# A two-block transformer kernel: second MLP, latents and output product with tokens in partitions

## The chip, the core and the metric

The kernel runs on one core of a Trainium2 chip. A core has a matrix engine (TensorE, PE in the rows; its weight loads are PEld), VectorE (DVE), ScalarE (ACT), GpSimd (POOL) and SyncE (SP), which issues most transfers. Each engine works through its own list of instructions in order; an instruction that waits holds back everything behind it on its engine. The metric is the device time of one execution in microseconds, median of several.

## The reference, cut to what matters

```python
def _mlp(h, w1, w2):
    a = jax.nn.relu(h @ w1)
    return (a * a) @ w2                                      # 1024 -> 4096 -> 1024
...
# end of the first block (two layers; tokens: 256)
        hx = hx + gx2 * _mlp(_modulate(hx, norm2_g[i], sx2, cx2), mlp_w1[i], mlp_w2[i])
    return _rms_norm(hx, final_g)
...
# second block, two layers
        mod = jax.nn.silu(c) @ w_ada[l] + b_ada[l]
        shift, scale, gate = jnp.split(mod, 3, axis=-1)
        h = x * (1.0 + scale[:, None, :]) + shift[:, None, :]
        (p_cq, p_ckv, p_kr, p_qb, p_kb, p_vb, p_qc, p_kc, p_vc,
         p_qi, p_ki, p_wi, p_gate) = jnp.split(h @ w_in[l], SPLIT_POINTS, axis=-1)
        cq = rms_norm(p_cq, q_norm_g[l])                     # 768 wide
        ckv = rms_norm(p_ckv, kv_norm_g[l])                  # 256 wide
        ...                                                  # mla, dilated and sparse attention
        y = jnp.concatenate([...], axis=-1) * jax.nn.silu(p_gate)
        sub = y @ w_out[l]
        x = layer_norm(ALPHA * x + (1.0 + gate[:, None, :]) * sub, ln_g[l], ln_b[l])
```

The sparse attention of a layer first scores all keys with eight small index heads (`p_qi`, `p_ki`, `p_wi`) and keeps the 64 best causal keys of each query.

## The kernel before

256 tokens are two tiles (t = 0, 1) of 128. Every product is made in three passes (`mm3`, L322 to L324): activations and weights are split in a high and a low part, and high·high, low·high and high·low are added in one accumulator. A weight piece of 128x1024 numbers arrives by DMA (`raw`, four buffers), ACT casts it to `whi` (L198) and DVE makes `wlo` (L201; keys that end in "+" on POOL instead); five buffers of each. The order in which pieces come is the list of `weight_plan`. `W.hold` names an instruction ahead of which no further `wlo` may be issued on DVE. A scheduler that places instructions by modelled times orders each engine's list, so that a piece's `wlo` can stand between two steps of a norm.

Activations stand with features in partitions (`hx`, `ahi`/`alo`: eight tiles of 128 features x 256 tokens) in most products: a weight block of 128x128 is stationary and 256 tokens move, or an activation block is stationary and 256 (384) weight columns move. The accumulators are PSUM banks: four of tag `mm`, two of `s`, one of `pt` and one of `om`.

The stages that the change touches, in order of time:

- `mlp(1)`, the second MLP: for each of eight groups of 512 hidden features two halves of the first product (`narrow`), a squared ReLU, then four weight pieces whose products go, 256 columns each, to eight accumulations that DVE adds to `hx` (`resid`, L837).
- `block2_start`: 16 transposes turn `hx` to `xa` (tokens in partitions, for the residual); squares on ACT, added on POOL, summed over partitions by PE (`sq_stats`, L748); the rsqrt, a broadcast by PE (L725); then eight steps of `modulate` (L757), each split in `ahi`/`alo` (L369, L370). POOL scales `xa` (L1427, L1428).
- `block2_layer`, twice: (layer 1 only: `vb`); `misc` and `qi` (the index projections); `indexer`: 16 score matmuls (L1441), the scores on DVE (L1446 to L1452), then 16 rounds of `max` and `match_replace` (L1456, L1457) and `sel` (L1459). Behind it stand the latents `b2c` (4 x 48 matmuls; copied to `craw`, L1537), their statistics (L748, L1540, L336 to L353) and `chi`/`clo` (L1546, L367/L368); then `qb`, `kb` (six projections), in layer 0 `vb`, and the ten attention pairs (`block2_pair`, L1473 to L1492), between which further projections stand.
- the gate `b2g` (L1647 to L1649, `yh` on ACT, `yl` on POOL L368), with the rows for gate, scale and shift: read from DRAM, broadcast over partitions, and finished on POOL (`row`, L705, L707; L1635 to L1637).
- the output product `b2o`: `out_tok` with 256 columns of a weight piece moving, then the layer norm of a tile (`finish`), whose result is transposed (L1685) and split (L1689, L1690) for layer 1. Then POOL finishes the residual rows (L1717, four times).

## Time and profile before

| | us |
|---|---|
| median of three runs | 1458.37 (1454.1 to 1460.74) |
| the profiled execution: run, span | 1461.6, 1459.8 |
| PE busy | 1391.7 (95%) |
| DVE busy | 1048.5 (72%) |
| ACT busy | 643.8 (44%) |
| POOL busy | 294.3 (20%) |
| mean granted clock | 0.977 |
| chain that ended last, PE's share | 77% |

The first MLP lasts until about 625, the second from 853 to 1033, layer 0 of the second block from there to 1250, layer 1 to the end. A row of the timeline gives start, duration, engine, line, operation, output<-input, shape, count and in brackets the idle time of the engine before it and what ended it. Matmuls overlap, so the distance of two starts is the pace, not the printed duration. A time in a row counts from the span's start.

### The profile page before, as it was taken

Reading aid. Unit: us, or ns where it says so; the run is one execution under the profiler, and the core shown is the slowest. Engines: PE = TensorE matmul, PEld = TensorE weight load, DVE = VectorE, ACT = ScalarE, POOL = GpSimd, SP = SyncE. Lnnn points to the kernel's source line nnn. Section 1 sums busy time; section 2 is a strip of 40 time slices with the busy share of each in tenths; the row PEclk is TensorE's granted clock in tenths of the full one; section 3 lists DMA queues with packets and bytes.
Section 4 is the critical chain, followed back from the end, with each engine's and each line's share of the span. In section 5 each row is a group of like instructions: output and inputs, shape, how many; then the busy total and the mean of one; then the engine's idle time right before and its main releaser. Section 6 shows DMA issues by size and latency. Waiting matters only on the chain.

```text
span 1459.8 us, 24691 instructions
## 1 busy us (share of the span) xinstructions
PE 1391.7 (95%) x9585; PEld 1208.6 (83%) x9585; DVE 1048.5 (72%) x1958; ACT 643.8 (44%) x1229; POOL 294.3 (20%) x281
## 2 busy tenths in 40 slices
...
GB/s 314 282 73 181 173 202 41 59 101 200 163 240 269 282 299 253 270 170 105 73 75 100 59 157 190 177 197 174 113 166 193 116 191 139 137 131 204 87 156 73
DMA packets 198116, 240.32 MB, mean 165 GB/s; under 512 B 21071, under 2 KB 178544, under 8 KB 198000
## 3 DMA queue, kind: packets, MB, share of 16 engines
...
q0 software_dynamic: 512, 0.02, 0.0%
...
## 4 chain that ended last, share of the span: by engine, by line
PE 77%; DVE 11%; DMA 4%; issue 3%; POOL 2%; ACT 2%; SPq 0%; ACTq 0%; DVEq 0%; POOLq 0%
PE mm L322 21%; PE mm L323 20%; PE mm L324 20%; DMA adaw<-in_ada_w 2%; DVE wlo L201 2%; PE om L1080 2%; PE s L1473 2%; PE pt L1065 1%; PE om L1490 1%; PE mm L502 1%; PE om L1333 1%; PE s L1014 1%; PE om L748 1%; PE pt L1484 1%; DVE acc L534 1%
## 5 line engine op out<-in xcount | busy, mean ns | idle before, releaser
L201 DVE TENSOR_TENSOR wlo<-raw,whi 128x1024 fp32r<-128x1024 f32 (+3 forms) x278 | 358.8, 1300 | 132.2 <-ACT whi L198 123.2
L198 ACT CAST whi<-raw 128x1024 fp32r<-128x1024 f32 (+3 forms) x282 | 289.2, 1035 | 334.5 <-PE mm L323 263.0
L322 PE MATMUL mm<-ahi,whi 128*128 128x256 f32 (+2 forms) x1232 | 398.5, 324 | 2.3 <-ACT ahi L369 2.3
L323 PE MATMUL mm<-alo,whi 128*128 128x256 f32 (+1 forms) x1232 | 395.1, 321 | 3.2 <-DVE alo L370 3.1
L324 PE MATMUL mm<-ahi,wlo 128*128 128x256 f32 (+1 forms) x1232 | 394.2, 321 | 0.0
L322 PEld LDWEIGHTS mm<-ahi,whi 128*128 128x128 f32 (+1 forms) x1232 | 237.5, 193 | 24.3 <-issue 3.9
L323 PEld LDWEIGHTS mm<-alo,whi 128*128 128x128 f32 x1232 | 237.4, 193 | 21.0 <-DVE alo L370 4.0
L324 PEld LDWEIGHTS mm<-ahi,wlo 128*128 128x128 f32 x1232 | 237.1, 193 | 18.5 <-issue 2.2
L322 PE MATMUL mm<-hid,whi 128*128 128x256 f32 (+1 forms) x544 | 179.4, 330 | 0.0
L323 PE MATMUL mm<-hid,whi 128*128 128x256 f32 (+1 forms) x544 | 178.8, 329 | 0.0
L324 PE MATMUL mm<-hid,wlo 128*128 128x256 f32 (+1 forms) x544 | 178.4, 328 | 0.0
L368 POOL TENSOR_TENSOR hid<-e,hid 128x512 fp32r<-128x512 f32 x48 | 78.0, 1626 | 417.1 <-ACT hid L367 417.1
L534 DVE SCALAR_TENSOR_TENSOR acc<-adaw,cst,acc 128x1024 f32<-128x1024 f32 x98 | 125.1, 1291 | 0.4
L322 PEld LDWEIGHTS mm<-hid,whi 128*128 128x128 f32 x544 | 103.0, 189 | 10.6 <-ACT whi L198 0.4
L324 PEld LDWEIGHTS mm<-hid,wlo 128*128 128x128 f32 x544 | 103.2, 190 | 10.0
L323 PEld LDWEIGHTS mm<-hid,whi 128*128 128x128 f32 x544 | 103.0, 189 | 9.6
L837 DVE SCALAR_TENSOR_TENSOR hx<-mm,cst,hx 128x256 f32<-128x256 f32 x160 | 72.4, 479 | 30.7 <-PE mm L324 30.4
L322 PE MATMUL mm<-whi,ahi 128*128 128x256 f32 (+1 forms) x192 | 57.4, 299 | 0.7 <-ACT ahi L1689 0.7
L324 PE MATMUL mm<-whi,alo 128*128 128x256 f32 (+1 forms) x192 | 56.1, 292 | 1.4 <-DVE alo L1690 1.4
L1136 ACT ACTIVATE e<-mm 128x512 f32<-128x512 f32 x48 | 28.7, 598 | 64.2 <-PE mm L324 62.2
L1138 DVE SCALAR_TENSOR_TENSOR e<-mm,e 128x512 f32<-128x512 f32 x48 | 32.9, 686 | 32.7 <-ACT e L1136 32.5
L323 PE MATMUL mm<-wlo,ahi 128*128 128x256 f32 (+1 forms) x192 | 55.9, 291 | 0.0
...
## 6 DMA issues: line engine op xcount, KB each, us to landing
raw<-in_mlp_w SPq DMA_DIRECT2D x128, 512.0 KB, 4.8
...
```

What stands on the lines that cost most here:

```text
L198: self.nc.scalar.copy(hi[:, :m], raw)
L201: (self.nc.gpsimd if on_pool else self.nc.vector).tensor_tensor(lo[:, :m], raw, hi[:, :m].bitcast(F32), op=OP.subtract)
L322: mm(ps, w[0], x[0], start=start, stop=False, skip_group_check=skip)
L323: mm(ps, w[0], x[1], start=False, stop=False, skip_group_check=skip)
L324: mm(ps, w[1], x[0], start=False, stop=stop, skip_group_check=skip)
L368: return (lo_eng or nc.vector).tensor_tensor(lo, t, hf, op=OP.subtract)
L534: V.scalar_tensor_tensor(acc, raw, s, acc, op0=OP.mult, op1=OP.add)
L837: self.nc.vector.scalar_tensor_tensor(h[m], ps, self.adaT[l][:, base + m, r:r + 1], h[m], op0=OP.mult, op1=OP.add)
L1080: nc.tensor.matmul(o[64 * hh:64 * hh + 64, cols(qt)], self.v[ab][:, 4 - nkt + i, cols(j // 2, 64)], PT[:, i, hh], start=i == 0, stop=i == ...
L1136: nc.scalar.activation(r, ps, AF.Relu)
L1138: V.scalar_tensor_tensor(t, ps, 0.0, r, op0=OP.max, op1=OP.mult)
L1473: nc.tensor.matmul(s[:, c0:c0 + n], qf(h, cols(qt)), kf(h, slice(0, n)), start=True, stop=True)
```

## The change

The MLP's and the second block's weight pieces become 256 rows x 512 columns. In `mlp1` a block of 128 hidden features x 128 tokens is stationary and 512 weight columns move, into four accumulators (two tiles x two halves) that stay open over all eight groups, in the four `mm` banks; the first product uses the two `s` banks. The residual `xt` is made token by token in the first group (the 16 transposes), gate, shift and scale come as broadcast rows, and their biases are added where the rows are made (`ada_jobs`: POOL fills a tile by up to 8 small DMAs, DVE adds, 4 to 8 small DMAs write the rows out). The last group and the final norm go tile by tile. In a layer of the second block, `b2c`, `vb` and `vc` come first, tokens stationary, 512, 384 and 256 columns moving; tile 1 follows tile 0 by three pieces (`LAG`). The latents' norm is worked per tile of tokens (squares on ACT, `latents`), and called behind `indexer`. The output product moves 512 columns, and `finish(t)` stands behind each tile's last product in both layers. `vb`'s low parts are made on DVE in both layers. The row additions of a layer (L705, L707) are gone.

```diff
-                for g in range(4):
-                    add(f"m{l}w2", w2, e * 512 - 512, 4, g * 256, 256)
+                for i in range(4):
+                    if l:
+                        add(f"m{l}w2", w2, e * 512 - 512 + 256 * (i // 2), 2, i % 2 * 512, 512)
...
+        for g in range(2):
             for i in range(4):
-                add("b2vb" + "+" * l, w, 256 * i, 2, 1824, 384)
+                add("b2c", w, 256 * i, 2, 512 * g, 512)
+        for i in range(4):
+            add("b2vb", w, 256 * i, 2, 1824, 384)
+        group("b2vc", w, 2720)
...
+                if rows:
+                    b = self.e([128, 256])
+                    nc.gpsimd.memset(b, 0.0)
+                    for i, key, bias in rows:
+                        for j in range(4):
+                            nc.gpsimd.dma_start(b[32 * j + i:32 * j + i + 1], bias[256 * j:256 * j + 256].unsqueeze(0))
+                    g2 = self.e([128, 256])
+                    nc.vector.scalar_tensor_tensor(g2, gt, plus, b, op0=OP.add, op1=OP.add)
...
-        nc.gpsimd.tensor_tensor(r, r, b, op=OP.add)
-        if plus:
-            nc.gpsimd.tensor_scalar(r, r, plus, 0.0, op0=OP.add, op1=OP.add)
...
+                self.mm3(acc[t][i % 2], (hh[:, kk, cols(t)], hl[:, kk, cols(t)]), (wh[:, k], wl[:, k]),
+                         e == 0 and kk == 0, e == 7 and kk == 3)
...
+            for i in (0, 2, 1, 3):
+                product(7, i, t, ws[i])
+            ss = self.sm([128, 2])
+            x = xt[t]
+            z = self.k4([128, 1024], name="z")
+            for i in range(2):
+                c = cols(i, 512)
+                V.tensor_tensor(z[:, c], acc[t][i], gate[:, c], op=OP.mult)
+                V.tensor_tensor(x[:, c], z[:, c], x[:, c], op=OP.add)
+                nc.scalar.activation(z[:, c], x[:, c], AF.Square, accum_out=ss[:, i:i + 1])
+            s1 = self.sm([128, 1])
+            V.tensor_tensor(s1, ss[:, 0:1], ss[:, 1:2], op=OP.add)
+            rstd = self.rsqrt(s1, 1, 1.0 / D, 1e-6, True)
+            for i in range(2):
+                c = cols(i, 512)
+                V.scalar_tensor_tensor(z[:, c], x[:, c], rstd, gr[:, c], op0=OP.mult, op1=OP.mult)
+                V.tensor_tensor(z[:, c], z[:, c], sr[:, c], op=OP.add)
+                self.turn_input(z[:, c], i, t, hi4, lo4)
+            with self.tc.issue_after(self.pow.ins):
+                nc.gpsimd.tensor_scalar(x, x, rstd, ALPHA, op0=OP.mult, op1=OP.mult)
+                nc.gpsimd.tensor_tensor(x, x, fr, op=OP.mult)
...
+    def turn_input(self, u, i, t, hi4, lo4):
+        nc = self.nc
+        pt = self.psum("pt", [128, 4, 128])
+        for k in range(4):
+            nc.tensor.transpose(pt[:, k], u[:, cols(k)], self.ident)
+        hv, lv = (f[i][:, :, cols(t)] for f in (hi4, lo4))
+        self.last_hi = nc.scalar.copy(hv, pt)
+        op = nc.vector.tensor_tensor(lv, pt, hv.bitcast(F32), op=OP.subtract)
+        if i == 0:
+            self.W.hold = op.ins
...
+        gain = self.k4([128, 1024], name="lgain")
+        self.after(gain, xa[0])
...
+        def token_step(i, t, w):
+            key, k0, nk, n = steps[i]
+            if k0 == 0:
+                pss[t, key] = self.psum("mm" if key < 2 else "s", [128, n])
+            ps = pss[t, key]
+            for k in range(nk):
+                kk = k0 + k
+                self.mm3(ps, (a[0][kk][:, cols(t)], a[1][kk][:, cols(t)]), (w[0][:, k], w[1][:, k]), kk == 0, kk == 7)
...
+                c = cols(key, 512)
+                V.tensor_tensor(lat[t][:, c], ps, gain[:, c], op=OP.mult)
+                junk = self.e()
+                for j in range(key + 1):
+                    cc = slice(256 * j, 256 * j + 512 // (key + 1))
+                    nc.scalar.activation(junk[:, cc], ps[:, cc], AF.Square, accum_out=cst[t][:, key + j:key + j + 1])
+        steps = ([(g, 2 * i, 2, 512) for g in range(2) for i in range(4)] + [(2, 2 * i, 2, 384) for i in range(4)]
+                 + [(3, 4 * i, 4, 256) for i in range(2)])
+        LAG, ws = 3, {}
+        for i in range(len(steps) + LAG):
+            if i < len(steps):
+                ws[i] = self.W.get(("b2c", "b2c", "b2vb", "b2vc")[steps[i][0]])
+                token_step(i, 0, ws[i])
+            if i >= LAG:
+                token_step(i - LAG, 1, ws.pop(i - LAG))
...
+            r = self.rsqrt(s[:, 0:2], 2, 1.0 / 256, 1e-6, True)
+            u = lat[t]
+            V.tensor_scalar(u[:, 0:768], u[:, 0:768], r[:, 0:1], None, op0=OP.mult)
+            V.tensor_scalar(u[:, 768:1024], u[:, 768:1024], r[:, 1:2], None, op0=OP.mult)
+            for i in range(2):
+                pt = self.psum("pt", [128, 4, 128])
+                for k in range(4):
+                    nc.tensor.transpose(pt[:, k], u[:, 512 * i + 128 * k:512 * i + 128 * k + 128], self.ident)
+                hv, lv = (f[i][:, :, cols(t)] for f in (chi4, clo4))
+                nc.scalar.copy(hv, pt)
+                V.tensor_tensor(lv, pt, hv.bitcast(F32), op=OP.subtract)
...
         sel = self.indexer(l, qi, ki, wi)
-        craw = [self.k4([128, 4, 256], name="craw") for _ in range(2)]
...
+        for t in range(2):
+            latents(t)
...
+            tmp = self.k4([128, 1024], name="tmp")
+            nc.gpsimd.tensor_tensor(tmp, lnb, gr, op=OP.mult)
+            nc.gpsimd.tensor_tensor(gr, lng, gr, op=OP.mult)
+            nc.gpsimd.tensor_tensor(sr, tmp, sr, op=OP.add)
...
-        for gg in range(2):
-            ws = [[self.W.get("b2o") for _ in range(2)] for _ in range(2)]
+        for g in range(2):
+            ws = [self.W.get("b2o") for _ in range(4)]
             for t in range(2):
-                for g in range(2):
-                    out_tok(2 * gg + g, t, ws[g], self.psum("mm", [128, 256]))
-                if gg == 1 and l == 0:
+                out_tok(g, t, ws)
+                if g:
                     finish(t)
         if l == 1:
-            finish(0)
-            finish(1)
```

Between the scores of the indexer and the attention pairs (layer 0). On PE before, behind the last score (`s`, L1441) stands the first latent product (`mm_10878`):

```order
L1441 MATMUL s_10810<-misc_10627,qi_10642 128x128 [waits PE_49]
L1441 MATMUL s_10810<-misc_10627,qi_10642 128x256
L1441 MATMUL s_10817<-misc_10627,qi_10642 128x128 [waits Activation_49]
L1441 MATMUL s_10817<-misc_10627,qi_10642 128x256
L322 MATMUL mm_10878<-ahi_10554,whi_10708 128x256
L323 MATMUL mm_10878<-alo_10556,whi_10708 128x256
L324 MATMUL mm_10878<-ahi_10554,wlo_10709 128x256
L322 MATMUL mm_10878<-ahi_10554,whi_10708 128x256
L323 MATMUL mm_10878<-alo_10556,whi_10708 128x256
```

On PE now, behind the scores stand the projections; the last of the fourth (`mm_10921`, `kb`), then the transposes of the latents (`lat`, L1594), then the fifth:

```order
L320 MATMUL mm_10921<-ahi_10052,whi_10853 128x256
L321 MATMUL mm_10921<-alo_10054,whi_10853 128x256
L322 MATMUL mm_10921<-ahi_10052,wlo_10854 128x256
L1594 MATMUL pt_10778<-cst_61,lat_10177 128x128 [waits DVE_49,Activation_49]
L1594 MATMUL pt_10778<-cst_61,lat_10177 128x128 x3
L1594 MATMUL pt_10785<-cst_61,lat_10177 128x128 [waits DVE_49]
L1594 MATMUL pt_10785<-cst_61,lat_10177 128x128 x3
L320 MATMUL mm_10953<-ahi_10051,whi_10885 128x256
L321 MATMUL mm_10953<-alo_10053,whi_10885 128x256
L322 MATMUL mm_10953<-ahi_10051,wlo_10886 128x256
L320 MATMUL mm_10953<-ahi_10051,whi_10885 128x256
L1594 MATMUL pt_10801<-cst_61,lat_10178 128x128 x4
```

The four latent products have moved from behind the scores to ahead of them, and transposes that wait for DVE stand between the fourth and the fifth projection.

On DVE before, at the end of the indexer (`score`, `sel`), the statistics of the latents follow:

```order
L1457 MATCH_REPLACE score_10767<-sm_10868,score_10767 128x256 [waits DVE_49]
L1456 MAX sm_10871<-score_10767 128x8 [waits DVE_49]
L1457 MATCH_REPLACE score_10767<-sm_10871,score_10767 128x256 [waits DVE_49]
L1459 TENSOR_SCALAR sel_10874<-score_10767 128x384 [waits DVE_49]
L201 TENSOR_TENSOR wlo_11262<-raw_11065,whi_11261 128x1024 [waits DMAHW1_49,PE_49,Activation_49]
L1540 TENSOR_SCALAR sm_11126<-om_11127 128x2 [waits PE_49]
L201 TENSOR_TENSOR wlo_11294<-raw_11095,whi_11293 128x1024 [waits DMAHW2_49,Activation_49]
L1540 TENSOR_SCALAR sm_11126<-om_11153 128x2 [waits PE_49]
L336 TENSOR_SCALAR sm_11163<-sm_11126 128x4 [waits DVE_49]
```

On DVE now, the scaling of the latents (`lat`, L1589, L1590) follows the last rounds, and `clo` (L1597) follows both tiles' scaling:

```order
L1495 MAX sm_10761<-score_10660 128x8 [waits DVE_49]
L1496 MATCH_REPLACE score_10660<-sm_10761,score_10660 128x256 [waits DVE_49]
L1495 MAX sm_10764<-score_10660 128x8 [waits DVE_49]
L328 TENSOR_SCALAR sm_10772<-sm_10179 128x2
L1496 MATCH_REPLACE score_10660<-sm_10764,score_10660 128x256 [waits DVE_49]
L1589 TENSOR_SCALAR lat_10177<-lat_10177,sm_10774 128x768 [waits Pool_49]
L1498 TENSOR_SCALAR sel_10767<-score_10660 128x384 [waits DVE_49]
L1590 TENSOR_SCALAR lat_10177<-lat_10177,sm_10774 128x256
L328 TENSOR_SCALAR sm_10795<-sm_10180 128x2
L1589 TENSOR_SCALAR lat_10178<-lat_10178,sm_10797 128x768 [waits Pool_49]
L1590 TENSOR_SCALAR lat_10178<-lat_10178,sm_10797 128x256
L1597 TENSOR_TENSOR clo_10487<-pt_10778,chi_10485 128x4x128 [waits Activation_49]
L1597 TENSOR_TENSOR clo_10488<-pt_10785,chi_10486 128x4x128 [waits Activation_49]
```

Ahead of both stands the whole indexer; what PE waits for now comes out of DVE's list behind it.

At the gate of layer 0, on POOL, before: the rows' additions stand among the low parts `yl`:

```order
L705 TENSOR_TENSOR rows_12324<-rows_12324,rowb_12325 128x1024 [waits DMAHW3_49,DMAHW2_49,Pool_49]
L707 TENSOR_SCALAR rows_12324<-rows_12324 128x1024 [waits Pool_49]
L1635 TENSOR_TENSOR gsr_12339<-lgb_12318,rows_12324 128x1024 [waits DMAHW4_49,PE_49,Pool_49]
L1636 TENSOR_TENSOR gsr_12340<-lgb_12319,rows_12324 128x1024 [waits DMAHW5_49,PE_49]
L1707 TENSOR_SCALAR lgb_12319<-lgb_12319 128x1024 [waits Pool_49]
L368 TENSOR_TENSOR yl_12346<-e_12409,yh_12344 128x256 [waits DVE_49,Activation_49]
L368 TENSOR_TENSOR yl_12346<-e_12415,yh_12344 128x256 [waits Activation_49]
L705 TENSOR_TENSOR rows_12332<-rows_12332,rowb_12333 128x1024 [waits DMAHW1_49,DMAHW0_49]
L368 TENSOR_TENSOR yl_12346<-e_12482,yh_12344 128x256 [waits Activation_49]
L1637 TENSOR_TENSOR gsr_12340<-gsr_12340,rows_12332 128x1024 [waits Pool_49]
L368 TENSOR_TENSOR yl_12346<-e_12488,yh_12344 128x256 [waits Activation_49]
L368 TENSOR_TENSOR yl_12347<-e_12555,yh_12345 128x256 [waits Activation_49]
L368 TENSOR_TENSOR yl_12347<-e_12561,yh_12345 128x256 [waits Activation_49]
```

On POOL now:

```order
L1695 TENSOR_TENSOR tmp_11778<-rows_11769,rows_11772 128x1024 [waits DMAHW7_49,DMAHW0_49,Pool_49]
L1696 TENSOR_TENSOR rows_11772<-rows_11766,rows_11772 128x1024 [waits DMAHW1_49,Pool_49]
L1697 TENSOR_TENSOR rows_11775<-tmp_11778,rows_11775 128x1024 [waits DMAHW1_49]
L366 TENSOR_TENSOR yl_11784<-e_11847,yh_11782 128x256 [waits PE_49,Activation_49]
L366 TENSOR_TENSOR yl_11784<-e_11853,yh_11782 128x256 [waits Activation_49]
L1756 TENSOR_SCALAR rows_11769<-rows_11769 128x1024
L366 TENSOR_TENSOR yl_11784<-e_11920,yh_11782 128x256 [waits Activation_49]
L366 TENSOR_TENSOR yl_11784<-e_11926,yh_11782 128x256 [waits Activation_49]
```

Three long row additions (L1695 to L1697) are left, all ahead of the first `yl`.

At the boundary from the second MLP to layer 0, on DVE before: `modulate` and the split by feature tile, one row of 256 tokens each:

```order
L757 SCALAR_TENSOR_TENSOR e_10566<-hx0_133,sm_10552,om_10549 128x256 [waits Activation_49]
L370 SCALAR_TENSOR_TENSOR alo_10556<-e_10558,cst_61,ahi_10554 128x256 [waits Activation_49]
L370 SCALAR_TENSOR_TENSOR alo_10556<-e_10562,cst_61,ahi_10554 128x256 [waits Activation_49]
L757 SCALAR_TENSOR_TENSOR e_10570<-hx0_133,sm_10552,om_10549 128x256
L757 SCALAR_TENSOR_TENSOR e_10574<-hx1_134,sm_10552,om_10549 128x256 [waits DVE_49]
L370 SCALAR_TENSOR_TENSOR alo_10556<-e_10566,cst_61,ahi_10554 128x256 [waits Activation_49]
L370 SCALAR_TENSOR_TENSOR alo_10556<-e_10570,cst_61,ahi_10554 128x256 [waits Activation_49]
L370 SCALAR_TENSOR_TENSOR alo_10557<-e_10574,cst_61,ahi_10555 128x256 [waits Activation_49]
L757 SCALAR_TENSOR_TENSOR e_10578<-hx1_134,sm_10552,om_10549 128x256
```

On DVE now: the end of tile 0's norm, all of tile 1's, and then the next pieces' low parts:

```order
L1236 TENSOR_TENSOR z_10080<-z_10080,rows_8564 128x512 [waits DVE_49] x2
L1251 TENSOR_TENSOR alo_10053<-pt_10095,ahi_10051 128x4x128 [waits Activation_49]
L1251 TENSOR_TENSOR alo_10054<-pt_10104,ahi_10052 128x4x128 [waits Activation_49]
L1227 TENSOR_TENSOR z_10138<-mm_8391,rows_8558 128x512
L1235 SCALAR_TENSOR_TENSOR z_10138<-xt_8530,sm_10149,rows_8567 128x512 [waits Pool_49]
L1235 SCALAR_TENSOR_TENSOR z_10138<-xt_8530,sm_10149,rows_8567 128x512
L1236 TENSOR_TENSOR z_10138<-z_10138,rows_8564 128x512 [waits DVE_49] x2
L1251 TENSOR_TENSOR alo_10053<-pt_10153,ahi_10051 128x4x128 [waits Activation_49]
L199 TENSOR_TENSOR wlo_10184<-raw_10033,whi_10183 128x1024 [waits DMAHW4_49]
L199 TENSOR_TENSOR wlo_10197<-raw_10039,whi_10196 128x1024 [waits DMAHW5_49]
L1251 TENSOR_TENSOR alo_10054<-pt_10162,ahi_10052 128x4x128 [waits Activation_49]
```

The norm of tile 1 stands behind that of tile 0, and the low parts of the third and fourth piece (`wlo_10184`, `wlo_10197`) behind tile 1's first `alo`.

## Rows read from the trace of the kernel before

**Rows 1.** Windows: stretch, length, each engine's busy time and instructions, clock, DMA share, GB/s.

```profile
416.30:438.60 22.30, 22.30 (x99) 18.00 (x97) 21.08 (x31) 5.85 (x8) 3.35 (x2) 1.00 0.74 238
900.00:1000.00 100.00, 100.00 (x844) 100.00 (x844) 65.43 (x82) 45.34 (x53) 15.85 (x9) 1.00 0.56 180
```

**Rows 2.** Windows, the same columns: from the scores of layer 1 to its first pair.

```profile
1287.00:1334.00 47.00, 46.72 (x400) 45.55 (x396) 40.85 (x104) 25.50 (x46) 11.25 (x11) 1.00 0.49 140
```

**Rows 3.** Timeline of PE: first scores of both layers, first pair of layer 1.

```profile
1063.17 0.93 PE L1441 MATMUL s<-misc,qi 64*128 64x128 f32 x8
...
1286.68 0.93 PE L1441 MATMUL s<-misc,qi 64*128 64x128 f32 x8
...
1334.02 0.49 PE L1473 MATMUL s<-qkb 64*128 64x128 f32 x4
```

**Rows 4.** Groups of DVE in 1066.2 to 1092.9: busy us, mean ns.

```profile
L201 DVE TENSOR_TENSOR wlo<-raw,whi 128x1024 fp32r<-128x1024 f32 x8 | 10.1, 1266 | 1.6 <-ACT whi L198 1.6
```

**Rows 5.** Timeline of DVE: the indexer's first and last operation, layer 0.

```profile
1066.28 0.55 DVE L1446 TENSOR_SCALAR score<-e,sm 128x128 f32<-128x128 f32 x2
...
1092.54 0.36 DVE L1459 TENSOR_SCALAR sel<-score 128x384 f32<-128x384 f32 x1
```

**Rows 6.** Groups of PE in 1286.6 to 1334.0: the scores.

```profile
L1441 PE MATMUL s<-misc,qi 64*128 64x128 f32 (+1 forms) x32 | 3.3, 340 | 0.0
```

**Rows 7.** Timeline: 512-wide steps of a norm on DVE, ACT and POOL.

```profile
1254.28 1.40 DVE L1676 SCALAR_TENSOR_TENSOR u<-z,sm,gsr 128x512 f32<-128x512 f32 x2
1258.94 0.59 ACT L1689 CAST ahi<-pt 128x512 fp32r<-128x512 f32 x1 [1.26 <-PE pt L1685]
1254.44 1.00 POOL L332 TENSOR_TENSOR sm<-sm,cst 128x1 f32<-128x1 f32 x1 [3.49 <-DVE sm L330]
```

**Rows 8.** Windows: before and after PE's longest idle time of layer 1's start.

```profile
1274.90:1280.70 5.80, 5.80 (x28) 4.99 (x29) 3.31 (x3) 1.05 (x1) 1.45 (x2) 0.58 0.38 122
1280.70:1286.60 5.90, 5.90 (x52) 5.85 (x50) 2.45 (x2) 3.54 (x4) 0.00 (x0) 1.00 0.68 188
```

**Rows 9.** Windows: MLP to layer 0, output product of layer 0, its norm, output product of layer 1.

```profile
1033.00:1063.00 30.00, 24.02 (x163) 22.22 (x161) 20.93 (x30) 14.16 (x24) 10.08 (x7) 0.77 0.18 51
1214.00:1250.00 36.00, 28.07 (x206) 26.86 (x205) 26.28 (x35) 11.49 (x19) 24.16 (x18) 0.86 0.39 107
1250.00:1287.00 37.00, 28.00 (x186) 25.80 (x186) 27.12 (x28) 15.67 (x21) 17.56 (x12) 0.91 0.49 147
...
1429.00:1452.00 23.00, 23.00 (x194) 22.84 (x193) 16.08 (x31) 4.83 (x8) 8.55 (x9) 1.00 0.08 29
```

**Rows 10.** Timeline of PE and POOL: gate rows of layer 0, and who waits.

```profile
1217.59 0.39 PE L324 MATMUL mm<-whi,yl 128*128 128x256 f32 x1 [2.07 <-POOL yl L368]
...
1221.75 0.58 PE L324 MATMUL mm<-whi,yl 128*128 128x256 f32 x1 [3.54 <-POOL yl L368]
...
1198.13 2.67 POOL L705 TENSOR_TENSOR rows<-rows,rowb 128x1024 f32<-128x1024 f32 x1 [4.90 <-DMA rowb<-in_b_ada]
1200.89 3.70 POOL L707 TENSOR_SCALAR rows<-rows 128x1024 f32<-128x1024 f32 x1
```

**Rows 11.** Timeline of POOL, DVE and PE: long POOL additions and what ran beside them.

```profile
1040.81 4.85 POOL L1428 TENSOR_TENSOR xa<-xa,fgrow 128x1024 f32<-128x1024 f32 x2
...
1041.06 4.88 DVE L370 SCALAR_TENSOR_TENSOR alo<-e,cst,ahi 128x256 fp32r<-128x256 f32 x2
...
1260.75 12.34 POOL L1717 TENSOR_TENSOR z<-z,lgb 128x1024 f32<-128x1024 f32 x4 [3.06 <-ACT z L1714]
...
1262.78 11.40 DVE L201 TENSOR_TENSOR wlo<-raw,whi 128x1024 fp32r<-128x1024 f32 x4 [2.52 <-ACT whi L198]
...
1274.89 1.06 PE L1724 MATMUL om<-misc,kc 32*32 32x256 f32 x2 [6.52 <-DVE sm L1525]
```

**Rows 12.** Timeline: the last column group's product on DVE; eight row DMAs on POOL.

```profile
1452.17 0.42 DVE L1664 TENSOR_TENSOR z<-mm,rows 128x256 f32<-128x256 f32 x1 [0.20 <-PE mm L324]
...
624.64 4.13 POOL L682 DMA_DIRECT2D row<-adag  x8 [19.19 <-ACT adag L544]
```

315 lines of the change are left out of this document (137 added, 178 removed).

## The prediction

> **What bounds the kernel now.** I read the windows first, since a share over the whole span says nothing of a stage. Inside the MLPs PE has no idle time and runs at full clock: 844 matmuls of 256 columns in 100 us, and 99 matmuls, nearly all of 512 columns, in 22.3 us [rows 1]. So there only PE's pace counts. The second block's layers are nearly as dense between the first scores and the first pair (46.72 of 47 us busy [rows 2]). Time is lost at three places: from the MLP to layer 0 (6 of 30 us idle, clock 0.77), around the output product of layer 0 (7.9 of 36 us idle, clock 0.86) and at layer 1's start (9 of 37 us idle, clock 0.91); the output product of layer 1 loses nothing [rows 9]. Such idle time costs twice: after a wait of 6.52 us [rows 11] the granted clock is 0.58 for 5.8 us, in which 28 matmuls go where 52 go in the next 5.9 us [rows 8], about 2.5 us more. I call T the start of PE's first score of a layer.
>
> **Parts that shorten. Wider matmuls:** 768 pairs of 256-column matmuls become one each (384 in the MLP, 192 in the latents, 192 in the output products). A pair takes 2 x 100/844 us = 0.237, one of 512 columns 0.232 on a run of 96 (by the window's 22.3/99, 0.225, as a few are smaller) [rows 1]: 5 ns each, **-4**; bounds -9 (0.225) and -2.
>
> The Trainium skill, page "TensorE: Matmul & The Clock Gate", section "Back-to-back issue gap", gives N/2.4 + 2.5 ns for a matmul of N columns, by which a pair would save 2.5 ns, so 2 us in all; the rows show both sizes slower than that. The same section has a sustained 131 ns at 512 columns, by which this part would save over 80 us and the kernel would end near 1377; the window's 22.3 us for 99 matmuls speaks against it, so it gets a chance of less than 1 in 100.
>
> **Gate rows.** 192 products of the output with all around them take 36 us in layer 0 and 23 in layer 1 [rows 9]. Of the 13, some 3 are the norm inside that stretch; 10 follow from the long row additions on POOL, which hold back `yl` (idle 2.07 and 3.54 us, and the low clock after them). Two additions and a scaling ahead of the first `yl` and one between them go (2.67, 3.70 and as much as 2.67 [rows 10]); three of about 2.4 us are left, which begin as the rows have landed, 1198 on this axis, and end some 7.5 us later, 9 us ahead of the first output product. I take **-8.5** (bounds -10 and -5), since wider products also reach the last `yl` sooner.
>
> **Tail.** Layer 1's last step on DVE works on 512 columns instead of 256: three operations of 0.70 [rows 7] for three of 0.42 [rows 12], **+0.8**. Tile 0's finish ends ahead of it either way.
>
> **Parts that move. MLP to layer 0.** The 16 residual transposes go into the MLP (16 x 0.12 = **+1.9** of PE there). Now 30 us hold 120 products of 0.119 (14.2), so 15.8 are lost [rows 9]. After: from the end of tile 0's product, tile 1's takes 24 x 0.232 = 5.6. Tile 0's norm on DVE: gate and residual of the second half 1.4, square 0.7, sums 0.3, a `wlo` 0.5 more, POOL's power 1.0, two scalings 1.4, then shifts 1.4 [rows 7]. But POOL's addition on the residual, 4.85/2 = 2.4, starts with them, and an operation of DVE with two SBUF inputs beside one took 4.88/2 instead of 0.42 [rows 11]: first transposes at 8.2 instead of 6. Tile 1's chain stands wholly behind it on DVE and meets the same: its first transposes come at about 20.8, while PE has run out at 13. The third and fourth pieces' `wlo` come behind that, and PE is steady from 27.4, having done 54 products (12.5): 14.9 lost, with 2.5 for the low clock 17.4, **+1.5** (bounds -4, without POOL's overlap, and +5).
>
> **Layer 0 to layer 1.** Now 37 us hold 48 products of 0.175 and 120 of 0.119 (22.6), so 14.4, and 3 us ahead of that: 17.4 lost. POOL makes no `wlo` any more, but its four additions (12.34) still hold DVE's `wlo` to 11.40/4 = 2.85 each [rows 11]. Worked out as above, PE is steady at 18.8 with 3.6 lost; then `lgain`, whose transfer waits for a POOL copy behind the third addition, lands about 31 and holds DVE's first latent row and the `wlo` behind it until 33, with 23.1 us of work done: 10 lost, with the products' starts and the clock 14. **-3** (bounds -11, if `lgain` is early, and +4).
>
> **Latent wait.** This is the largest term. Now the latent products, 192 of 0.119 = 22.8, stand behind the scores and cover the indexer on DVE, which lasts from T + 3.1 for 26.6 us [rows 3, 5]. After, only `qb` and three quarters of what follows stand there. PE: scores 3.3 [rows 6], four projections 96 x 0.119 = 11.4, so T + 14.7; then the transposes of `lat`. DVE: in the 26.6 us are six `wlo` of 1.27 (7.6 [rows 4]) and two copies like those of 0.70 (1.4 [rows 7]); 17.6 is the indexer. After, four `wlo` (5.1) stand in it, and tile 0's scaling comes behind the last round: 3.1 + 17.6 + 5.1 - 0.4 + 0.6 (768 columns, between 0.36 for 384 and 0.70) = T + 26.0. PE waits 11.3. The four turns share the one `pt` bank: each is 0.5 on PE, 0.59 on ACT and 0.70 on DVE [rows 7], and the first low part stands behind tile 1's scaling too, so they start at 26.0, 28.1, 29.9 and 31.7. Seventeen of the last 48 products fit between; 31 are left (3.7): first pair at T + 35.9, with the low clock T + 38.4. Work in it is 3.3 + 144 x 0.119 + 2.0 = 22.4, so 13.5 to 16 are lost. Against now: T to pair is 47.3 [rows 3], less 22.8 for the moved products leaves 24.5. So 11.4 to 13.9 per layer; layer 1's list reads the same. I take 13.5, **+27** for both (bounds +16, if the rounds need less and the clock stays, and +32). What could cover it, the attention pairs' own projections, stands behind the transposes on PE's list.
>
> **Smaller.** `vb` and `vc` only move (their products are as before). With tile 1 three pieces behind, four of five weight buffers are held; a freed one needs ACT 1.05 and DVE 1.27 plus waits, about 2.5, against 12 x 0.232 = 2.78 of products: hidden, but a latent row of 0.70 in between takes the rest; **+2** for both layers (0 to +6). The ada rows: bias DMAs like those of 0.5 us each [rows 12], most beside an MLP in which PE alone counts; the last four jobs' writes stand among the squares of a norm on POOL, **+1** (0 to +4).
>
> **Sum:** -4 - 8.5 + 0.8 + 1.9 + 1.5 - 3 + 27 + 2 + 1 = +18.7 on the profiled run's 1461.6, so 1480; that run lies 3.2 above the median of 1458.4, on whose scale I state **1477** (own range 1464 to 1490).
>
> **Rivals.** *The stalls' relief outweighs the latent wait (faster).* At the three lossy places the wait now ends on a long POOL addition. If DVE and PE there pass it (`lgain` early, POOL's additions not beside the norms), the terms are -4, -11 and -10 with -7 for the matmuls, and the latents stay at +16 as the rounds go back to back: -4 - 11 - 10 - 7 + 16 + 6 = -10, **1448**. It decides from about 24 us of gain at these places. For it: the rows show those losses really are there to be had; against it: all three still have a POOL addition beside DVE on the new list.
>
> *The wait is there but half covered (about the same).* If the four turns overlap and the clock recovers within the wait, 9 per layer: 18.7 - 9 = +9.7, and the boundaries at half their bounds give 9 back: **1459**. For it: ACT and DVE are otherwise free there.
>
> *Every piece waits (slower still).* If the lag leaves one free buffer while POOL holds DVE, a step takes 1.05 + 2.85 + waits, 4.1, against 2.78 for some eight steps in layer 1 and half of that in layer 0: +15 on the sum, **1490**.
>
> *The change does not do what it says:* the lists show fewer matmuls and the new order, so no chance of its own.
>
> **How the numbers follow.** Forecast 0.60, faster rival 0.18, same 0.14, slower still 0.08. About 0.5% (7.3 us) is what a measurement can tell from no change. Faster takes the first rival's 0.18, less its nearest part, 0.17; same 0.17, with the forecast's low edge; slower 0.66. The range reaches from 1450, half into the faster rival, to 1490.
>
> **What would show it.** In the new profile: PE idle of 9 to 13 us in each layer, put down to DVE's scaling of `lat` (L1589), at transposes L1594, and a clock near 0.6 behind it; the indexer on DVE about as long as now. The idle on `yl` gone. A first transposes' idle of about 7 us in tile 1 of the MLP's norm. 512-column matmuls at 0.232. The forecast is wrong if the scaling of `lat` stands free of the indexer, or if the first pair begins before T + 31.

## The result, and the profile after

The changed kernel takes 1475.5 us (median of four runs, 1473.97 to 1476.02) against 1459.41 for the kernel before beside it: a ratio of 1.012 with a 95% interval of 1.009 to 1.015. It is slower, 1.5 us from the forecast of 1477. The profiled execution took 1476.02 with a span of 1474.2, against 1461.6 and 1459.8 before, so 14.4 more. In the page PE is busy 8.8 us less than before (1382.9 for 1391.7) but stands still 23 us longer, and its mean granted clock is lower (0.970 for 0.977): PE waits longer and then runs slow.

First the windows of the changed kernel by stage, the columns as in [rows 1]: the second MLP; from it to layer 0's scores; scores to first pair; pairs to the output product; output product and norm to layer 1's scores; scores to first pair; pairs to the output product; its own stretch.

```profile
851.07:1034.74 183.67, 182.28 (x1163) 165.93 (x1164) 99.75 (x101) 90.29 (x113) 33.51 (x23) 0.98 0.60 195
1034.74:1102.68 67.94, 60.22 (x335) 51.84 (x333) 40.51 (x52) 27.36 (x48) 11.60 (x8) 0.90 0.56 157
1102.68:1140.76 38.08, 25.62 (x193) 24.04 (x192) 28.45 (x83) 13.28 (x24) 1.71 (x4) 0.82 0.27 82
1140.76:1229.31 88.55, 86.97 (x648) 72.58 (x648) 62.88 (x160) 48.00 (x122) 29.54 (x29) 1.00 0.45 147
1229.31:1317.99 88.68, 79.64 (x430) 66.79 (x428) 56.61 (x72) 38.81 (x60) 27.40 (x19) 0.98 0.58 167
1317.99:1355.95 37.96, 25.38 (x194) 23.81 (x193) 28.46 (x83) 13.39 (x24) 1.41 (x2) 0.82 0.20 65
1355.95:1442.92 86.97, 86.24 (x647) 72.52 (x647) 56.59 (x161) 49.27 (x125) 19.62 (x24) 1.00 0.45 146
1442.92:1464.70 21.78, 21.78 (x97) 17.84 (x96) 13.99 (x21) 4.82 (x8) 7.28 (x7) 1.00 0.07 25
```

The two rows from scores to first pair stand out: 12.5 us without work for PE in each, at a clock of 0.82, where the kernel before had next to none [rows 2]. The same borders in the trace of before:

```profile
848.10:1033.00 184.90, 184.84 (x1536) 184.55 (x1536) 121.66 (x156) 87.43 (x109) 32.20 (x23) 0.99 0.59 187
1033.00:1063.17 30.17, 24.19 (x164) 22.25 (x162) 21.10 (x30) 14.16 (x24) 10.08 (x7) 0.77 0.18 52
1063.17:1121.04 57.87, 57.29 (x449) 55.77 (x449) 45.36 (x109) 29.40 (x52) 9.15 (x13) 0.97 0.55 162
1121.04:1214.40 93.36, 92.22 (x696) 78.30 (x696) 65.60 (x160) 49.06 (x124) 38.71 (x34) 1.00 0.54 178
1214.40:1286.68 72.28, 55.36 (x382) 51.95 (x380) 52.94 (x61) 26.89 (x37) 41.33 (x28) 0.88 0.44 126
1286.68:1334.02 47.34, 47.06 (x402) 45.88 (x401) 41.01 (x104) 25.71 (x46) 11.25 (x11) 1.00 0.50 142
```

Products moved across these borders, so only stretches that hold the same work before and after can be set side by side. The second MLP's first product begins at 848.1 before, not at the 853 given above. The last column adds the prediction's terms by stretch, rounded:

| stretch | before | after | difference | by the prediction's terms |
|---|---|---|---|---|
| start to the second MLP's first product | 848.1 | 851.1 | +3.0 | +1 |
| second MLP | 184.9 | 183.7 | -1.2 | 0 |
| MLP's end to layer 0's output product | 181.4 | 194.6 | +13.2 | +15.5 |
| from there to layer 1's output product | 214.7 | 213.6 | -1.1 | +2 |
| that product and the tail | 30.7 | 31.3 | +0.5 | +0.3 |
| sum | | | +14.4 | +18.8 |

The waits of PE in the whole of the changed kernel (engine and line that waits, what ended the wait; total, how often, longest; waits of the first MLP and of the start left out):

```profile
PE pt L1594 <- DVE lat L1589: 21.3, 2, 10.7
PE mm L321 <- DVE wlo L199: 6.5, 4, 5.4
PE pt L1248 <- DVE z L1236: 5.9, 2, 4.6
...
PE pt L1594 <- DVE clo L1597: 3.7, 2, 1.9
```

The first line is the forecast's largest term. In the timeline of the changed kernel, PE's transposes of layer 0 and what DVE did ahead of them:

```profile
1126.65 0.41 DVE L1496 MATCH_REPLACE8 score<-sm,score 128x256 f32<-128x256 f32 x1
...
1127.50 0.62 DVE L1589 TENSOR_SCALAR lat<-lat,sm 128x768 f32<-128x768 f32 x1 [0.44 <-POOL sm L330]
...
1128.26 1.09 PE L1594 MATMUL pt<-cst,lat 128*128 128x128 f32 x4 [10.61 <-DVE lat L1589]
...
1131.20 1.12 PE L1594 MATMUL pt<-cst,lat 128*128 128x128 f32 x4 [1.85 <-DVE clo L1597]
```

and the windows behind that wait, up to the first pair at 1140.76:

```profile
1128.20:1134.00 5.80, 3.88 (x17) 3.51 (x18) 2.79 (x7) 2.23 (x6) 1.00 (x3) 0.50 0.00 0
1134.00:1140.00 6.00, 6.00 (x44) 6.00 (x43) 2.44 (x3) 2.33 (x5) 0.00 (x0) 0.78 0.50 153
```

DVE's last round of the indexer ends, 0.44 us later the power from POOL is there, `lat` is scaled, and PE starts after 10.61 us of nothing. The clock is then 0.50, the lower of its two levels (1.2 of 2.4 GHz), and comes back within the second window. PE's waits on `yl`, 2.07 and 3.54 us in [rows 10], are down to 0.2.

### The profile page after: what moved, and what is told of

Read it like the earlier page. It is cut to its first block, busy times and chain, and to the rows that moved or that the text cites. A ratio compares the mean times of both kernels' runs of the same rounds, so it can differ in the third digit from the quotient of the medians.

```text
span 1474.2 us, 23024 instructions
## 1 busy us (share of the span) xinstructions
PE 1382.9 (94%) x8779; PEld 1166.3 (79%) x8779; DVE 1016.8 (69%) x1879; ACT 639.2 (43%) x1221; POOL 270.7 (18%) x290
## 4 chain that ended last, share of the span: by engine, by line
PE 74%; DVE 13%; DMA 4%; issue 3%; POOL 3%; ACT 2%; SPq 0%; ACTq 0%; DVEq 0%; POOLq 0%
PE mm L320 17%; PE mm L321 17%; PE mm L322 17%; PE s L321 3%; PE s L322 3%; PE s L320 3%; DVE wlo L199 2%; PE om L1074 2%; DMA adaw<-in_ada_w 2%; PE s L1512 1%; PE pt L1059 1%; PE om L1529 1%; PE mm L499 1%; PE om L1400 1%; ACT whi L197 1%
## 5 line engine op out<-in xcount | busy, mean ns | idle before, releaser
L320 PE MATMUL mm<-ahi,whi 128*128 128x256 f32 (+1 forms) x848 | 288.1, 340 | 0.0
L321 PE MATMUL mm<-alo,whi 128*128 128x256 f32 (+1 forms) x848 | 285.0, 336 | 0.0
L322 PE MATMUL mm<-ahi,wlo 128*128 128x256 f32 (+1 forms) x848 | 284.8, 336 | 0.0
L320 PEld LDWEIGHTS mm<-ahi,whi 128*128 128x128 f32 x848 | 164.0, 193 | 20.4 <-issue 3.6
L322 PEld LDWEIGHTS mm<-ahi,wlo 128*128 128x128 f32 x848 | 163.3, 193 | 18.2 <-issue 2.4
L321 PEld LDWEIGHTS mm<-alo,whi 128*128 128x128 f32 x848 | 163.6, 193 | 16.0 <-issue 1.8
L320 PE MATMUL mm<-hid,whi 128*128 128x512 f32 (+1 forms) x288 | 106.7, 371 | 0.0
L321 PE MATMUL mm<-hid,whi 128*128 128x512 f32 (+1 forms) x288 | 106.0, 368 | 0.0
L322 PE MATMUL mm<-hid,wlo 128*128 128x512 f32 (+1 forms) x288 | 105.9, 368 | 0.0
L320 PE MATMUL s<-ahi,whi 128*128 128x256 f32 x256 | 73.1, 286 | 1.2 <-ACT ahi L367 1.2
L320 PEld LDWEIGHTS mm<-hid,whi 128*128 128x128 f32 x288 | 54.1, 188 | 10.2 <-issue 0.4
L321 PEld LDWEIGHTS mm<-hid,whi 128*128 128x128 f32 x288 | 54.2, 188 | 9.2
```

What stands on the lines that cost most here:

```text
L320: mm(ps, w[0], x[0], start=start, stop=False, skip_group_check=skip)
L321: mm(ps, w[0], x[1], start=False, stop=False, skip_group_check=skip)
L322: mm(ps, w[1], x[0], start=False, stop=stop, skip_group_check=skip)
```

## The experiments

Each is timed against the kernel before on its own chip (1458.98 to 1459.44 there). Three other orders around the indexer come first, then edits at the other waits of the changed kernel, then the halves of a wide matmul and one edit of the kernel before, and last the combinations and the ada rows. "By the medians" compares the median times; "by the profiles" compares single profiled executions from the first product of the first MLP on, since that product began anywhere from 300.4 to 306.7 us. By that measure the kernel before takes 1155.8, the changed one 1170.4.

**Latents ahead of the indexer.** Only the call moves:

```diff
+        for t in range(2):
+            latents(t)
         sel = self.indexer(l, qi, ki, wi)
-        for t in range(2):
-            latents(t)
```

> The changed kernel with one thing moved: the latents' norm (scaling, transposes, split) is called ahead of the indexer instead of behind it. Theory (the latent wait is the indexer on DVE standing ahead of the scaling): the first score to the first pair of a layer takes 24 to 27 us instead of 38, the idle time ahead of the latents' transposes falls from 10.6 to under 2 us per layer, and the kernel takes 1475.5 less 2 x 11 to 13.5, 1448 to 1454. Rival (the time sits in the lag of tile 1, the low clock or the four turns of the one transpose bank, and the order on DVE only shows where it waits): the wait comes back ahead of the scores or between the turns, at least half of it stays, 1463 or more.

Measured: 1456.09, 0.998 of the kernel before (0.9962 to 0.9999), so 19.4 less than the changed kernel by the medians and 21.6 by the profiles (1148.8). The wait on `lat` is gone. Waits of PE, from the second MLP's end on:

```profile
PE pt L1248 <- DVE z L1236: 6.5, 2, 5.2
PE mm L321 <- DVE wlo L199: 6.3, 4, 5.5
PE s L1512 <- DVE sm L1513: 3.2, 2, 1.6
```

The loss is the place of the scaling on DVE's list, behind the indexer, and not the new shape of the products. From the first score to the first pair a layer now takes 23.8 us, just under the expected 24 to 27, for 38.1 and 38.0. In layer 0:

```profile
1097.20:1121.00 23.80, 23.29 (x189) 21.12 (x188) 22.55 (x67) 12.68 (x24) 0.29 (x2) 1.00 0.45 141
```

Of these 28.4 us for both layers 8.0 come back between the first pair and the output product (93.3 and 90.2 us for 88.6 and 87.0): the indexer's last rounds now run on DVE beside the first pair, whose maxima (`sm`, L1513) stand among them. PE waits 1.6 us for those in each layer, and in layer 0 its clock is 0.84 behind that wait. So the kernel gains 19 to 22 us and ends 2 above the expected range; the forecast had 27.

**Indexer ahead of the latent products.** The index projections, their weight pieces and the indexer come first in a layer, and the latent products, `vb` and `vc` behind them, as a cover for DVE:

```diff
+        wh, wl = self.W.get("b2misc")
...
+        for g in range(2):
+            nc.scalar.copy(qi[:, 2 * g:2 * g + 2], self.narrow("b2qi", a))
+        sel = self.indexer(l, qi, ki, wi)
         steps = ([(g, 2 * i, 2, 512) for g in range(2) for i in range(4)] + [(2, 2 * i, 2, 384) for i in range(4)]
...
-        sel = self.indexer(l, qi, ki, wi)
```

> The changed kernel with the index projections and the indexer put back ahead of the latent products, as in the kernel before; widths, tiles and lag stay. Theory (order alone made the wait, 512 columns did not): the indexer is covered by 50 us of products again, 1448 to 1456. Rival (with four accumulators whose release stands among the indexer's rounds on DVE, the token-stationary form cannot cover the indexer): PE waits on the accumulators or the low parts, 1463 or more.

Measured: 1451.57, 0.9946 (0.9927 to 0.9966), 24 less than the changed kernel and faster than the one before. The same wait can be removed from the other side, by putting work over the indexer again. The longest waits left here lie at the two borders, 7.8 us on `z` (L1236) and 4.4 on `u` (L1740): both tiles' norms must be through before a product of all 256 tokens starts. A single wait of 3.2 on ACT's `qi` stands ahead of the scores.

**Values first, latents behind the scores.** A mixture of the two: `vb` and `vc` ahead of the index projections, `b2c` between the scores and the rest.

```diff
+        run([(2, 2 * i, 2, 384) for i in range(4)] + [(3, 4 * i, 4, 256) for i in range(2)], 3)
...
         sel = self.indexer(l, qi, ki, wi)
+        run([(g, 2 * i, 2, 512) for g in range(2) for i in range(4)], 3)
```

> The changed kernel in another order: only the two value projections stand ahead of the index projections, and the latent products, 44 us with the projections behind them, stand behind the scores again. Theory (the norms' edge needs some token-stationary products, the indexer needs the rest behind it): both latent waits go (27 us) and the wait for the gain row too (6): 1440 to 1446, faster than both kernels and than either latents_first or indexer_first. Rival (384 columns a step cover the norms less than 512 do, and the accumulators wait among the indexer's rounds): at best indexer_first, 1450 or more.

Measured: 1455.15, 0.998 (0.9962 to 0.9997): a miss by 9 to 15 us. The wait on `lat` is 0.9 at most, but a new one of 7.5 us took its place, in layer 1 alone. PE waits there for ACT's copy of `misc`. This copy stands on ACT's list behind casts of weight pieces that came late: SP issued their transfers behind the gain row's, and held that one 10.1 us for a copy on POOL. The expectation counted the gain row's wait as gone; it came back on another path. A wait of PE and one of SP's list, and ACT's timeline:

```profile
PE om L1612 <- ACT misc L1607: 7.5, 1, 7.5
SPq L1541 <- POOL lgain L358: 10.1, 1, 10.1
...
1270.30 1.04 ACT L197 CAST whi<-raw 128x1024 fp32r<-128x1024 f32 x1 [9.62 <-DMA raw<-in_w_in]
...
1274.17 0.36 ACT L1607 COPY misc<-mm 104x256 f32<-104x256 f32 x1
```

The next edit is aimed at that copy; the two were not run together, so what this order is worth without the gain row's wait is open.

**Layer 1's gain row.** Its buffer's fill (POOL, a copy of one number that the row's transfer waits for) is bound to the second tile's `rstd` instead of to the residual behind the additions:

```diff
-        self.after(gain, xa[0])
+        self.after(gain, self.gdep if l else xa[0])
...
+            self.gdep = rstd
```

> The changed kernel with one wait taken away: the latents' gain row of layer 1 is loaded as soon as the second tile's rstd is there, no longer behind POOL's third residual addition. Theory (that transfer holds DVE's first latent row for 6.64 us, and with it the low parts behind it): the wait of 5.45 us on PE before layer 1's third latent step falls to 1 to 2 us, its low clock goes, 4 to 7 us gained: 1469 to 1472. Rival (POOL's four additions hold the low parts anyway): 0 to 2 us gained, 1473 or more, the wait now on low parts of 2.5 us each.

Measured: 1466.58, 1.0053 (1.0032 to 1.0073), 8.9 less than the changed kernel by the medians and 7.1 by the profiles, more than expected. In the stretch that the edit is aimed at, from layer 0's output product to layer 1's scores, it is the expected size: 83.5 us for 88.7, so 5.2. In the changed kernel the copy stood between the third and fourth long addition on POOL, the row landed late, and DVE and PE waited one behind the other. Timeline of the changed kernel, POOL, DVE and PE:

```profile
1263.87 10.15 POOL L1766 TENSOR_TENSOR z<-z,rows 128x1024 f32<-128x1024 f32 x3 [3.80 <-ACT z L1763]
1273.96 0.17 POOL L358 COPY lgain<-z 1x1 f32<-1x1 f32 x1
...
1278.40 0.69 DVE L1563 TENSOR_TENSOR lat<-mm,lgain 128x512 f32<-128x512 f32 x1 [6.64 <-DMA lgain<-in_q_norm_g]
...
1280.28 0.79 PE L321 MATMUL mm<-wlo,ahi 128*128 128x512 f32 x1 [5.45 <-DVE wlo L199]
```

With the edit DVE starts the first latent row at 1261.53, and the longest wait of PE on `wlo` is 0.7:

```profile
1261.53 0.69 DVE L1563 TENSOR_TENSOR lat<-mm,lgain 128x512 f32<-128x512 f32 x1 [0.26 <-PE mm L322]
```

**The same without POOL's long additions.**

```diff
-        for o, row in ((OP.mult, lng), (OP.add, lnb)):
-            for x in z:
-                nc.gpsimd.tensor_tensor(x, x, row, op=o)
```

> As e5_lgain, and POOL's four residual additions at the end of layer 0 are left out as well (that part of the computation is missing). If the gain row was all, nothing is left to win: the same as e5_lgain within 1 us. If the additions hold DVE's low parts as in the kernel before (2.85 us each), 2 to 4 us more than e5_lgain.

Measured: 1462.89, 1.003 (1.001 to 1.005), 3.7 less than with the gain row alone by the medians and 1.9 by the profiles (1163.3, 1161.4). The stretch from layer 0's output product to layer 1's scores takes 80.4 for 83.5. So the additions beside DVE cost some 2 to 4 us, and the row bound to the third of them about twice that.

**Tile 1's gate ahead of tile 0's turn.** At the end of the second MLP `z`, `xt` and the squares of tile 1 are called before the transposes and low parts of tile 0:

```diff
...
+        gated(0)
+        r0 = scaled(0)
+        gated(1)
+        rest(0, *r0)
+        rest(1, *scaled(1))
```

> The changed kernel with DVE's list at the end of the second MLP in another order: tile 1's gate and residual (four operations, 2.6 us) stand ahead of tile 0's low parts instead of behind them. Theory (the 4.58 us that PE waits there for tile 1's transposes is DVE's list, not PE or POOL): tile 1's transposes come 2 to 3 us earlier, the wait falls to about 2, and 2 to 4 us are gained: 1471.5 to 1473.5. Rival (tile 0's low parts come later by the same and PE waits for them): no gain, 1475 or more.

Measured: 1468.16, 1.0062 (1.0039 to 1.0085), 7.3 less by the medians and 5.4 by the profiles, more than expected. The transposes of tile 1 come 11.0 us behind the MLP's last product instead of 12.8 and wait 0.57 for `z` instead of 4.58, and the stretch to layer 0's scores runs at a clock of 0.95 instead of 0.90 and takes 63.08 instead of 67.94. So some 2 us are the order and about 3 come with the clock; in kernels where nothing was changed in it, this stretch took 65.4 to 68.0, so not all of the 4.9 need be the edit's. Timeline of this kernel, POOL and DVE:

```profile
1037.38 2.36 POOL L1250 TENSOR_TENSOR xt<-xt,rows 128x1024 f32<-128x1024 f32 x1
...
1037.97 2.33 DVE L1229 TENSOR_TENSOR xt<-z,xt 128x512 f32<-128x512 f32 x1
```

An addition of DVE on 512 columns that takes 0.69 alone takes 2.33 here, and ends 0.56 behind POOL's (1040.30 and 1039.74). The Trainium skill, page "SBUF — State Buffer", section "SBUF: two separate sides", says that a DVE operation with two inputs in SBUF and a GpSimd operation that reads SBUF exclude each other for a whole instruction; this row agrees. [rows 11] had shown the same pair.

**Halves.** Each 512-column matmul as two of 256 into the same accumulator:

```diff
+            for h in range(2):
+                c = slice(256 * h, 256 * h + 256)
+                mm(ps[:, c], w[wi], x[xi][:, c], start=first and h == 0, stop=last, skip_group_check=True)
```

> The changed kernel with each 512-column matmul of the second MLP, the latents and the output product given as two of 256 columns into the same accumulator: 768 matmuls more, nothing else. By the rows of the changed kernel (48 matmuls of 512 columns in 10.96 us, 96 of 256 columns in 11.31) a pair costs 7 to 8 ns more than one: +5.5 to 6.5 us, 1481 to 1482. By the prediction's term +4, 1479.5. By the Trainium skill's gap of 2.5 ns per matmul (page TensorE: Matmul & The Clock Gate, section Back-to-back issue gap): +2, 1477.5.

Measured: 1478.83, 1.0132 (1.01 to 1.0164): 3.3 more than the changed kernel by the medians, but 0.9 by the profiles. Two windows of the changed kernel give the pace directly, 96 matmuls of 256 columns of the first product and 48 of 512 (the counts include the ones at the edges); the third is the whole second MLP of this kernel, to be set beside the 183.67 us of the changed one:

```profile
890.20:901.51 11.31, 11.31 (x97) 11.31 (x96) 5.50 (x5) 5.20 (x6) 1.74 (x1) 1.00 0.59 190
901.51:912.47 10.96, 10.96 (x50) 9.01 (x49) 5.50 (x5) 6.17 (x7) 1.82 (x1) 1.00 0.57 188
...
851.88:1038.82 186.94, 185.53 (x1546) 185.04 (x1547) 99.99 (x101) 90.43 (x113) 29.75 (x23) 0.98 0.58 192
```

That is (11.31 - 10.96)/48 = 7 ns for a pair by the windows. The second MLP, in which PE hardly waits, settles it: 3.3 us for its 384 pairs, 8.5 ns each. For all 768 pairs that makes some 6.5 us, an estimate from this stretch. The whole kernel's difference falls short of it; this kernel's longest wait on `wlo` is 2.5 instead of 5.4.

**The kernel before without row additions** (and without the loads of the bias rows).

```diff
-        nc.gpsimd.tensor_tensor(r, r, b, op=OP.add)
-        if plus:
-            nc.gpsimd.tensor_scalar(r, r, plus, 0.0, op0=OP.add, op1=OP.add)
```

> The kernel before with only the row additions of the gate stage left out (bias row and plus one, on POOL, and the loads of the bias rows; that part of the computation is missing). Theory (they hold back the low parts of the gate in layer 0): the idle time of 5.6 us ahead of the output product and the low clock behind it go, 1459.4 less 8.5 to 10, about 1450. Rival (the rest of POOL's row work, three additions and a scaling, holds them back alone): less than 4 us gained, 1456 or more.

Measured: 1450.35, 0.9936 (0.9912 to 0.9959): 8.6 less than the kernel before by the medians, 7.8 by the profiles. 6.4 of it lie in the stretch from layer 0's output product to layer 1's scores (65.9 for 72.3), where PE's waits on `yl` fall from 6.3 to 1.6. This is the gate rows' term of -8.5, or a little less, taken out of the other kernel by itself.

**All three edits.** Latents ahead, gain row, gate early:

> The changed kernel with three edits at once: the latents' scaling and transposes ahead of the indexer, layer 1's gain row loaded after the second tile's rstd, and tile 1's gate and residual ahead of tile 0's low parts at the end of the second MLP. If the three waits are separate losses, their gains add: 1475.5 - 19.4 - 8.9 - 7.3 = 1440, so 1436 to 1445, some 18 faster than the kernel before, and the wider products are then worth having. Rival: the losses hand over to one another (DVE has the same work at the three places, so a wait that is taken away at one comes back at the next), then 1449 or more.

Measured: 1447.59 (1447.12 to 1449.37), 0.9916 (0.9895 to 0.9937): 11.9 faster than the kernel before, 27.9 below the changed one. The single gains add to 35.6, so 7.7 are missing, and the time lies between the two expectations. The hand-over that the rival speaks of doesn't show in the waits. PE's longest, from the second MLP's end on:

```profile
PE s L1528 <- DVE sm L1529: 3.2, 2, 1.7
PE mm L320 <- ACT ahi L1266: 2.8, 4, 0.7
PE pt L1264 <- DVE z L1242: 2.7, 2, 2.2
PE mm L321 <- DVE wlo L199: 2.3, 4, 1.3
```

In its profile 3.1 of the missing lie in one stretch of layer 1, that of the first pairs. The windows hold the same work: layer 0 and layer 1 of the kernel with the latents ahead alone, then layer 1 of this one:

```profile
1121.00:1141.90 20.90, 19.31 (x105) 13.85 (x104) 11.46 (x50) 8.06 (x27) 1.95 (x2) 0.84 0.46 148
1327.70:1345.60 17.90, 16.25 (x105) 11.38 (x104) 11.42 (x50) 8.00 (x27) 1.96 (x2) 1.00 0.67 213
...
1322.90:1343.90 21.00, 19.35 (x106) 13.91 (x105) 11.96 (x50) 8.09 (x27) 1.96 (x2) 0.84 0.57 182
```

All three have one wait of 1.6 to 1.65 us ahead of the same matmul; behind it the clock fell in two of them and not in the third. Another 2.2 lie between the second MLP and layer 0 (63.52 us, where the sum of the two gains would give 61.3), at a clock of 0.95. And the gain row and the early gate gave 5.2 and 4.9 in their own stretches, not the 8.9 and 7.3 of the medians that the 35.6 is added from; why the medians gave more is open.

**Indexer first, with the other two edits.**

> The same, but with the index projections and the indexer ahead of the latent products, as the kernel before has them, in place of the latents ahead of the indexer. With that order the latent rows come late in a layer and the gain row cannot hold them, so the second edit should give 0 to 2 here and the third its 7: 1451.6 - 7 - 1 = 1443, so 1440 to 1447, level with the other combination. Rival: the gain row's transfer holds the low parts in this order too, then 1434 to 1438.

Measured: 1451.54, 0.9945 (0.9927 to 0.9963), the same as the indexer first alone: the gain row gives nothing, as expected, but neither does the early gate. The second transposes come 11.0 us behind the MLP's last product; without the two edits they came 10.7 behind it. In that order PE has both halves of tile 0 to turn at once (no product stands between them), so tile 0's low parts held tile 1's chain on DVE for their own 1.3 us only, and the early gate puts one of its operations beside POOL (2.35 for 0.69). Timeline of PE, first without the two edits, then with them:

```profile
1036.35 1.26 PE L1248 MATMUL pt<-cst,z 128*128 128x128 f32 x8 [1.29 <-DVE z L1236]
1045.38 1.09 PE L1248 MATMUL pt<-cst,z 128*128 128x128 f32 x4 [7.77 <-DVE z L1236]
...
1036.08 0.77 PE L1264 MATMUL pt<-cst,z 128*128 128x128 f32 x4 [2.17 <-DVE z L1242]
1038.31 1.11 PE L1264 MATMUL pt<-cst,z 128*128 128x128 f32 x4 [1.46 <-DVE alo L1267]
1044.49 1.08 PE L1264 MATMUL pt<-cst,z 128*128 128x128 f32 x4 [5.07 <-DVE z L1242]
```

**The ada rows, in two.** First without the bias loads, then with the rows' writes on SP's queue:

```diff
-                    nc.gpsimd.memset(b, 0.0)
...
-                            nc.gpsimd.dma_start(b[32 * j + i:32 * j + i + 1], bias[256 * j:256 * j + 256].unsqueeze(0))
...
-                    nc.vector.scalar_tensor_tensor(g2, gt, plus, b, op0=OP.add, op1=OP.add)
+                    nc.vector.tensor_scalar(g2, gt, plus, None, op0=OP.add)
```

> The changed kernel without the small transfers that load the biases of the rows (the biases are left out of the rows, the write of the rows stays). The trace has these loads beside the first MLP, where only PE counts, so the theory is that they cost nothing: 0 to -1 us against the changed kernel, 1474 to 1476, and first MLP's start to the next layer's start stays at 364 to 365 us. Rival: they hold POOL's low parts of the hidden features and are the 3 us by which the ada rows were undersized: 1472 and 361.5.

```diff
-                            nc.gpsimd.dma_start(d[j:j + 1], g2[32 * j + i:32 * j + i + 1])
+                            nc.sync.dma_start(d[j:j + 1], g2[32 * j + i:32 * j + i + 1])
```

> The changed kernel with the small transfers that write the rows out issued on SP's queue instead of POOL's; nothing is left out. In the trace the last job's writes stand between the squares' additions of the norm behind the first MLP on POOL, 0.5 us each, and the power behind them comes 2.7 us later than before. If these writes are the missing 3 us: -2 to -3.5, 1472 to 1473.5, and 361 to 362.5 us from the first MLP's start to the next layer's start. Rival: that stretch is held by something else (the writes fill idle time), -0.5 to +1, or weight loads behind the writes on SP come late, above 1476.

From the first MLP's first product to the next layer's first product of 512 columns the kernel before took 361.5 us and the changed one 364.6; the other kernels with its ada rows took 364.3 to 365.1. Without the bias loads it is 364.2, with the writes on SP 361.6: the writes are the 3 us, the loads next to nothing. Timeline of POOL in the changed kernel, then with the writes on SP, from the squares behind the first MLP to the power:

```profile
636.17 0.48 POOL L681 DMA_DIRECT2D row<-e  x1 [0.68 <-ACT e L730]
...
641.51 1.96 POOL L681 DMA_DIRECT2D row<-e  x4
644.06 0.71 POOL L330 TENSOR_TENSOR sm<-sm,cst 128x2 f32<-128x2 f32 x1 [0.59 <-DVE sm L710]
...
636.58 4.05 POOL L737 TENSOR_TENSOR sqa<-sqa,e 128x256 f32<-128x256 f32 x4
641.57 0.71 POOL L330 TENSOR_TENSOR sm<-sm,cst 128x2 f32<-128x2 f32 x1 [0.94 <-DVE sm L710]
```

The kernel times moved further than the stretch: 1470.47 (1.0068, 1.0047 to 1.0089) with the writes on SP and 1468.72 (1.0064, 1.0042 to 1.0086) without the loads, so 5.0 and 6.8 less than the changed kernel and both below the ranges expected. In the profiles the largest other piece is MLP to layer 0: 65.39 and 65.78 us against 67.94, at clocks of 0.95 and 0.92 against 0.90, with nothing changed in it. What made the kernel without the loads 6.8 us faster is not shown. A difference of that size between the medians of these variants is therefore no proof of anything by itself; the stretch is.

## Why the prediction was right

The size of the change was right, and its sign for the reason given. That the time came within 1.5 us is partly luck: on the profiled run the sum gave 1480, 4 us above the 1476.0 measured there. The forecast was put on the median's scale, 3.2 us under the profiled run of the kernel before, while the changed kernel's profiled run lies only 0.5 above its median.

**The latent wait** decided the sign, and its mechanism was read correctly: PE's transposes wait for DVE's scaling behind the indexer, 10.61 us by the timeline for 11.3 in the sum. `lat` was predicted at T + 26.0 and PE's transposes began at 25.6 (1128.26 - 1102.68); the clock fell as assumed, and the first pair came at T + 38.1 for 38.4. Against the layer's work before, that is the 13.5 for layer 1 (38.0 - 24.5). For layer 0 the term was too large. It took layer 1's list for both, but layer 0 had `vb` (48 matmuls of 0.175, 8.4) between scores and pairs: 57.87 - 22.8 - 8.4 = 26.7, so the wait cost 11.4 there. So the two waits cost 24.9 for the 27, which is 2 of the 4 us by which the sum was too high.

**Gate rows and the border to layer 1**, -8.5 and -3, with the matmuls and half the lag -11.5: the trace has 88.68 us where before 72.28 and 28.5 of moved products stood, -12.1. The single test gave -8.6 for the rows. The gain row was predicted to hold DVE until 33 us after tile 0's product, and PE's matmul behind it started 33.4 after it (1280.28 against 1246.9). The wait was in the sum, within the 14 us put down as lost there; the experiment took 5.2 of them away in this stretch.

**MLP to layer 0**, +1.5 with half of the lag and of the latents' matmuls +2, measured +0.9 (67.9 us where 30.2 and 36.9 of moved products stood). The predicted overlap of POOL with the first norm didn't occur: POOL's scaling writes `xt`, which DVE's second scaling still reads, so it started 1.67 us later than its power was ready, and its long operation with two inputs came after DVE's shifts. DVE was held elsewhere, by ACT's `ahi` behind PE's second transposes, and tile 1's chain stood behind that. PE's idle time at tile 1's transposes is 4.58 us for the 7 of the prediction's sign. That the stretch came out near its term is partly luck: its path was not the one worked out, and it varied by up to 2.6 us in kernels where nothing was changed in it.

**Wider matmuls**, 5 ns a pair predicted, 7 by the windows and 8.5 by the halves, inside the bounds: mis-sized by some 2.5 us. The second MLP gained 1.2 in spite of the 16 transposes. The Trainium skill's sustained 131 ns at 512 columns (page "TensorE: Matmul & The Clock Gate", section "Back-to-back issue gap") is not seen: 10.96/48 is 228 ns. With the prediction's other terms left in, that price would have ended near 1400 and not at its 1377.

**The ada rows** were the term that was mis-sized most for its size: +1, measured +3.0, inside its bound of 4. The step that failed is the sentence that put the last jobs' writes among the squares and counted little for it. Four writes of 0.5 us each between the additions, and four more ahead of the power, where before three stood, are all on the chain of that norm.

**Tail** +0.8, measured +1.6, less 1.0 for the output product ahead of it, which had -0.5: each is about twice its term, and the two together are +0.5 for +0.3. **Lag** +2: but for the wait that the gain row made, PE waits for a weight's low part 1 us in both layers together, at their starts. **No term** stood for layer 1's pairs, which took 2.4 less than before without `vc` (86.97 for 95.04 - 5.7); half of that is less idle time of PE (0.7 for 1.9). Layer 0's pairs took 0.9 more. Layer 1's pairs, layer 0's wait and the MLP's matmuls make the sum too high by some 6, the ada rows too low by 2.

The rival that the relief at the three lossy places outweighs the wait had the latents at +16, measured 24.9, and passed POOL's additions by at all three places, which the changed kernel does not: `lgain` was late. With the wait gone the kernel stands about level with the one before, and with two of the three places mended it is 11.9 us faster. That this is the 1448 that the rival named is chance, since the rival got there with +16 of the wait still in it. The rival in which every piece waits did not occur; its +15 on the sum would be 1492, not 1490.
